# Value rows of an expert layer placed by running sums of work, and a first block that goes ahead to its experts alone

## The chip, the core and the metric

The kernel runs on one core of a Trainium2 chip. The metric is the device time of one execution in microseconds. Five instruction streams run side by side: TensorE (PE in the profile; PEld is its loading of weights), VectorE (DVE), ScalarE (ACT), GpSimd (POOL) and SyncE (SP). Each works through its own instructions in the order in which they stand in the program, and waits for the others by semaphores. Transfers are issued by SP (weights, keys) and by POOL (gathers) and run on 16 DMA engines.

## What is computed

A decoder trunk of two layers over 512 tokens of width 1024. Each layer has a token mixer (differential attention and a recurrent branch, merged and projected), a layer norm, a lookup of experts, and another layer norm:

```python
for l in range(DEPTH):
    mix = token_mixer(x, w_in[l], ..., w_out[l], lam_init)
    x = layer_norm(DEEPNORM_ALPHA * x + mix, ln1_g[l], ln1_b[l])
    ffn = peer(x, peer_wq[l], peer_subkeys[l], peer_u[l], peer_v[l])
    x = layer_norm(DEEPNORM_ALPHA * x + ffn, ln2_g[l], ln2_b[l])

def peer(x, ...):
    q = (xt @ peer_wq).reshape(T, PEER_HEADS, 2, D_KEY_HALF)
    sc = einsum('thcd,hcnd->thcn', q, peer_subkeys)      # 8 heads, two halves of a key
    s1, i1 = top_k(sc[:, :, 0], 16); s2, i2 = top_k(sc[:, :, 1], 16)
    ...                                                  # best 16 of the sums: expert numbers e, weights g
    act = gelu(einsum('cd,ced->ce', xc, take(peer_u, ec)))
    out = einsum('ce,ced->cd', gc * act, take(peer_v, ec))
```

For each token 8 heads choose 16 experts each, so 128 rows of `peer_u` and 128 rows of `peer_v` are read per token and layer.

## The kernel before

**Tiles.** The tokens are four blocks of 128, one token per partition. A dense stage (mixer, then the choice of experts) takes two blocks together: blocks 0 and 1, then 2 and 3, in layer 0 and then in layer 1, so there are four dense stages. The experts run block by block, eight block passes in all, each of 128 gathers. One gather (line 728) brings, for each of the 128 tokens, one row of `peer_u` and the same row of `peer_v`: 1 MB into one of eight buffers `uvt`. The gathers are 1024 in number. They are counted from 0 below, so that gathers 0 to 127 belong to the first block pass, 128 to 255 to the second, and so on.

**One expert row.** VectorE forms the dot product of the token with the u half (line 731), two rows make a pair, ScalarE takes the pair through the gelu (lines 739 and 741), VectorE makes the two weights `w` (lines 743 and 694). Then the v half times its weight is added to the block's result, in one of two ways: VectorE adds it to `acc` (line 701), or ScalarE spreads the weight on a diagonal `dg` (line 705, two buffers) and TensorE multiplies the row with it into `pv` (line 707). Whichever reads the v half last frees the buffer. Which way a row goes is set while the program is written: `used[0]` grows by `self.share` per row, and where it reaches 1 the row goes to VectorE. The share stands in `PLAN` (line 55) for the mixer and for the choice of each dense stage, and is 0.5 where the experts run alone.

**The order.** Three streams are written into one program: `gathers` (experts), `dense` (mixer and choice of a stage) and `late` (the choice for the second block of a stage). `PLAN` gives for each dense stage the gather numbers between which its steps are laid out, so dense work of the next stage stands between the rows of the present block pass. The tile framework then orders the instructions of each engine by that and by the buffers.

**The first dense stage** has no gathers beside it, since the first experts are chosen at its end. Its weights and activations are split into a rounded part and a rest (`hi`, `lo`) and multiplied in three fast passes (`proj_T`, `proj_N`, `split_weight`). Behind the merge of the two branches come, for both blocks together, the output product (`proj_N`, line 550), layer norm (line 559), transposition (line 563) and then `route`: per half key a product with `peer_wq`, also in three passes, a product with the keys (line 587), the best 16 (`top16`) and, after a head, `choose`. `HGS` says how many heads are taken at a time.

## Time and profile before

| what | us |
|---|---|
| median of 3 runs | 3518.49 (3517.03 to 3527.47) |
| the profiled execution | 3519.91 |
| its span | 3518.2 |
| start of the first gather | 317.1 |
| start of the last block pass | 3182.8 |

The page gives busy times of the engines over the whole span. A share of the whole span mixes stages with different limits, so the stretches are what to read: the dense stage without gathers (to 317 us), three mixers beside experts, three ends of a choice beside experts, and the experts alone (from 2843 us). "GB/s" is what all DMA engines moved in a stretch. "PEclk" is the granted TensorE clock of the stretch, as a share of 2.4 GHz.

### The profile page before, as it was taken

To read this page: it belongs to the slowest core of one execution; us is meant where nothing else is said; L and a number is where in the kernel's file an instruction comes from. 1 tells how busy PE (TensorE), PEld (TensorE's weight loads), DVE (VectorE), ACT (ScalarE), POOL (GpSimd) and SP (SyncE) were. 2 spreads that over 40 slices of the span, in tenths; PEclk is the share of its full clock that TensorE was granted. 3 is DMA by queue.
4 is the path that set the end of the run, shared out by engine and by line. 5 is a ranking of instruction groups with operands and counts; after the bars stand their busy time and mean duration, and the time that the engine had idled before them with its cause. 6 is when DMAs were issued, how large, how long until landed. Compare 5 with 4: busy or idle time off the path is not lost.

```text
span 3518.2 us, 38040 instructions
## 1 busy us (share of the span) xinstructions
PE 2743.9 (78%) x11092; PEld 1791.3 (51%) x11092; DVE 2985.2 (85%) x7468; ACT 1267.1 (36%) x3510; POOL 1370.2 (39%) x1033
## 2 busy tenths in 40 slices
PE   8996887799987788896877697798987565556555
PEld 7995555567754365663754264575755221111111
DVE  7765999998799799978799789997789977778777
ACT  7842334443132354423222344443222232223222
POOL 0001234344333443444443434443443445554553
PEclk9997988899998899997989898899989787777776
DMA  5554799999999999999998999999999899999997
GB/s 202 161 168 173 284 379 359 370 415 417 418 402 371 361 405 397 389 418 384 418 395 335 412 399 366 388 402 414 404 410 353 309 374 421 421 421 407 422 421 304
DMA packets 219119, 1290.54 MB, mean 367 GB/s; under 512 B 24592, under 2 KB 37136, under 8 KB 87840
## 3 DMA queue, kind: packets, MB, share of 16 engines
q0 software_dynamic: 147456, 1073.81, 75.8%
q1 hardware_dynamic: 71456, 214.30, 16.2%
q8 instruction: 90, 1.47, 0.2%
q14 instruction: 117, 0.96, 0.1%
HBM read 1285.92 MB, written 2.10 MB: 366 GB/s over the span
## 4 chain that ended last, share of the span: by engine, by line
DVE 37%; PE 25%; DMA 14%; issue 12%; POOL 6%; ACT 6%; POOLq 0%; SPq 0%; DVEq 0%; ACTq 0%
DVE uvt L731 13%; DMA uvt<-uv_dram,e 13%; PE ps_mm L222 12%; DVE acc L701 9%; POOL uvt L728 6%; PE pv L707 6%; PE ps_mm L244 2%; ACT q L741 2%; DVE ef L667 1%; PE ps_ln L299 1%; DVE oh L665 1%; DMA sk<-spk_dram 1%; DVE oh L662 1%; DVE si L627 1%; DVE sc L630 1%
## 5 line engine op out<-in xcount | busy, mean ns | idle before, releaser
L728 POOL DMA_INDIRECT uvt<-uv_dram,e x1024 | 1367.7, 1336 | 2115.7 <-DVE acc L701 985.7
L707 PE MATMUL pv<-uvt,dg 128*128 128x512 f32 x1876 | 1137.7, 746 | 532.7 <-ACT dg L705 531.3
L731 DVE SCALAR_TENSOR_TENSOR uvt<-uvt,xn 128x1024 f32<-128x1024 f32 x1024 | 1243.6, 1219 | 93.7 <-DMA uvt<-uv_dram,e 75.1
L707 PEld LDWEIGHTS pv<-uvt,dg 128*128 128x128 f32 x1876 | 398.4, 229 | 1144.4 <-ACT dg L705 786.0
L222 PE MATMUL ps_mm<-room_xT,w 128*128 128x256 f32 x3072 | 723.1, 385 | 9.7 <-ACT qT L333 4.8
L701 DVE SCALAR_TENSOR_TENSOR acc<-uvt,w,acc 128x1024 f32<-128x1024 f32 x555 | 710.6, 1280 | 9.3
L222 PEld LDWEIGHTS ps_mm<-room_xT,w 128*128 128x128 f32 x3072 | 580.9, 193 | 138.5 <-issue 40.2
L739 ACT ACTIVATE q<-dots 128x2 f32<-128x2 f32 x512 | 103.7, 203 | 1220.5 <-DVE uvt L731 1218.1
L741 ACT ACTIVATE q<-q,dots 128x1 f32<-128x1 f32 x1024 | 341.0, 379 | 14.6
L694 DVE SCALAR_TENSOR_TENSOR w<-q,w 128x2 f32<-128x2 f32 x512 | 80.7, 158 | 233.4 <-ACT q L741 232.0
L705 ACT ACTIVATE dg<-ident,w 128x128 f32<-128x128 f32 x469 | 181.5, 399 | 200.5 <-DVE w L694 180.2
L222 PE MATMUL ps_mm<-room_xT,wsp 128*128 128x256 f32 x768 | 115.2, 293 | 28.7 <-ACT wsp L206 21.8
L207 DVE TENSOR_TENSOR wsp<-raw,wsp 128x1024 fp32r<-128x1024 f32 x96 | 116.2, 1221 | 17.9 <-ACT wsp L206 17.7
L222 PEld LDWEIGHTS ps_mm<-room_xT,wsp 128*128 128x128 f32 x768 | 101.1, 193 | 34.3 <-ACT wsp L206 22.8
L206 ACT CAST wsp<-raw 128x1024 fp32r<-128x1024 f32 x96 | 98.8, 1047 | 26.2 <-issue 7.5
L299 PE MATMUL ps_ln<-lnrows,ident 16*128 16x512 f32 x96 | 65.9, 812 | 39.2 <-DVE w L743 22.8
L244 PEld LDWEIGHTS ps_mm<-w,room_xT 128*128 128x128 f32 x768 | 90.6, 192 | 7.5 <-issue 4.8
L244 PE MATMUL ps_mm<-w,room_xT 128*128 128x128 f32 x768 | 92.7, 276 | 0.4 <-ACT tha L454 0.3
L244 PEld LDWEIGHTS ps_mm<-w,room_m 128*128 128x128 f32 x768 | 88.0, 192 | 7.3 <-issue 4.8
L222 PE MATMUL ps_mm<-room_ya,w 128*128 128x256 f32 x384 | 90.0, 382 | 1.5 <-DVE mth L506 1.2
L350 PE MATMUL s<-kT,qT 64*128 64x256 f32 (+1 forms) x384 | 71.1, 407 | 24.8 <-DVE pr L354 21.1
L244 PE MATMUL ps_mm<-w,room_m 128*128 128x128 f32 x768 | 88.6, 275 | 1.8 <-DVE room_m L510 1.1
(193 smaller groups left out, 2967.5 us busy)
## 6 DMA issues: line engine op xcount, KB each, us to landing
w<-wpk_dram SPq DMA_DIRECT2D x288, 512.0 KB, 8.3
raw<-wpk_dram SPq DMA_DIRECT2D x96, 512.0 KB, 4.4
uvt<-uv_dram,e POOLq DMA_INDIRECT x1024, 11.4
gw<-gpk_dram SPq DMA_DIRECT2D x32, 128.0 KB, 6.8
sk<-spk_dram SPq DMA_DIRECT2D x64, 64.0 KB, 7.1
xn<-x_dram SPq DMA_DIRECT2D x4, 512.0 KB, 4.0
out_dram<-xn SPq DMA_DIRECT2D x8, 256.0 KB, 6.1
lq<-lqk_dram SPq DMA_DIRECT2D x2, 128.0 KB, 6.7
```

The costliest lines, as they stand in the source:

```text
L206: self.nc.scalar.copy(hi, raw)
L207: self.nc.vector.tensor_tensor(lo, raw, hi.bitcast(F32), ALU.subtract)
L222: self.nc.tensor.matmul(ps[:, :n], w, x, start=i == 0, stop=i == len(steps) - 1)
L244: self.nc.tensor.matmul(out[:, i], x(slice(i * P, (i + 1) * P)), w, start=j == 0, stop=j == len(steps) - 1)
L299: nc.tensor.matmul(ps[:, half], self.ident[:16, r : r + 1].to_broadcast([16, P]), self.lnrows, start=True, stop=True)
L701: nc.vector.scalar_tensor_tensor(out=acc, in0=t[:, D:], scalar=w[:, i : i + 1], in1=acc, op0=ALU.mult, op1=ALU.add)
L705: nc.scalar.activation(dg, self.ident, AF.Copy, scale=w[:, i : i + 1])
L707: nc.tensor.matmul(pv[:, half], dg, t[:, D + half * 512 : D + (half + 1) * 512], start=not used[1], stop=j == P - 2)
L728: nc.gpsimd.indirect_dma_start(out=t, out_offset=None, in_=self.uv, in_offset=bass.IndirectOffsetOnAxis(ap=e[:, j : j + 1], axis=0))
L731: nc.vector.scalar_tensor_tensor(out=t[:, :D], in0=t[:, :D], scalar=C_GELU, in1=x, op0=ALU.mult, op1=ALU.mult, accum_out=dots[:, i : i + 1])
L739: nc.scalar.activation(q, dots, AF.Square, scale=A_GELU / C_GELU)
L741: nc.scalar.activation(q[:, k : k + 1], q[:, k : k + 1], AF.Tanh, scale=dots[:, k : k + 1], bias=dots[:, k : k + 1])
```

## The change

**Placement of value rows.** The shares in `PLAN` and the counter `used[0]` are gone. A class `Load` walks over the instructions written so far and keeps running sums for TensorE, VectorE and DMA, each instruction with a price by its size. DMA sets a floor: neither engine's sum may fall more than 8 us behind the sum of DMA, and the sum of DMA not more than 12 us behind the larger of the two. A row goes to VectorE where VectorE's sum plus 1.22 us is not above TensorE's sum plus 1.72 us. In the built order 699 of the 1024 rows go to TensorE in place of 469. VectorE keeps 325 in place of 555.

**First block alone.** In the first dense stage `first_experts` takes the place of the shared tail. The output weights are split for all eight chunks ahead, into all eight buffers of the gathers. The norm's scale and shift rows are brought by TensorE ahead of the product, into two PSUM tiles. Then block 0 goes alone through product, norm, transposition, the scores of head 0 and its choice. Block 1 follows with the same weights.

**Keys in float32.** The activations for the scores of that stage are kept in one float32 copy, and `peer_wq` is read as it is: 8 passes of float32 in place of 24 of the split form per half key, and no splitting of these 16 weight chunks.

```diff
-    (0, [2, 3], 30, 222, 270, 370, (0.7, 0.25)),
+    (0, [2, 3], 30, 222, 270, 370),
...
-V_ALONE = 0.5
...
-HGS = {True: (1, 1, 2, 2, 2), False: (2, 2, 2, 2)}
+HGS = {True: (1, 2, 2, 2), False: (2, 2, 2, 2)}
...
+class Load:
+    SLACK, AHEAD = 8.0, 12.0
...
+            if inst.engine == mybir.EngineType.PE:
+                self.pe += 0.013 + n / 2400 if inst.ins[0].dtype == F32R else 0.009 + n / 596
+            elif inst.engine == mybir.EngineType.DVE:
+                n = max([n] + [size(o) for o in inst.ins if hasattr(o, "ap")])
+                self.dve += 0.15 + n / 960 + 0.08 * (len(inst.outs) > 1 or "Match" in name)
+            elif name == "InstDMACopy":
+                self.dma += n * min(P, list(inst.outs[0].ap)[0][1]) * 4 / 420e3
+                self.dma = max(self.dma, max(self.pe, self.dve) - self.AHEAD)
+                self.pe = max(self.pe, self.dma - self.SLACK)
+                self.dve = max(self.dve, self.dma - self.SLACK)
...
+    def first_experts(self, l, blocks, m, sums):
+        nc = self.nc
+        affine = [self.norm_rows(l, 0, 0, self.ps_s, "s2"), self.norm_rows(l, 0, 1, self.ps_v, "pv")]
+        junk = self.ap.tile([P, D], F32, name="junk", tag="ya")
+        wts = []
+        for c in range(0, KC, 2):
+            t = [self.gp.tile([P, 2, D], F32R, name="wsp", tag="uv") for _ in range(2)]
+            for a in range(2):
+                self.split_weight(t[0][:, a], t[1][:, a], l, CH_OUT + c + a)
+            wts.append([v.rearrange("p a (k c) -> p a k c", k=KC) for v in t])
+        self.acts_x = Acts(self.room("xT"))
+        w = sk = None
+        for i, b in enumerate(blocks):
...
+            self.layer_norm(l, 0, [(b, sums[:, i, :2])], 4.0 * LN_EPS, junk, affine)
+            self.transpose_x(self.acts_x, i, b)
...
+            for c in range(2):
+                yield from self.score(l, c, w[c], sk[c], [i], sc)
+                o = [sv, si] if i == 0 else self.top
+                self.top16([(sc[i][:, c], o[0][:, c], o[1][:, c])])
+            if i == 0:
+                yield from self.choose(l, 0, 1, sv, si, b)
...
-                used[0] += self.share
-                if j == P - 1 or (used[0] >= 1.0 and j < P - 2):
-                    used[0] -= 1.0
+                self.load.update()
+                vector = self.load.dve + 1.22 <= self.load.pe + 1.72
+                if j == P - 1 or (vector and j < P - 2):
```

TensorE at the end of the first dense stage, before. The names: `wsp` are split weights, `room_uv` the merged activations, `ps_ln` the norm's rows, `ps_xt` the transposition (`xn_103` blocks 0 and 1, `xn_4775` blocks 2 and 3 of the next stage), `ps_sc` the scores.

```order
L244 MATMUL ps_mm<-wsp,room_uv 128x256 x192
L299 MATMUL ps_ln<-lnrows,ident 128x512 x2
L272 MATMUL ps_xt<-ident,xn_103 128x128 x16
L222 MATMUL ps_mm<-room_xT,wsp 128x256 x8
L222 MATMUL ps_mm<-room_kT_117,wsp 128x256 x8
L222 MATMUL ps_mm<-room_xT,wsp 128x256 x8
L272 MATMUL ps_xt<-ident,xn_4775 128x128 x4
L587 MATMUL ps_sc<-sk,pqT 128x128 x2
L222 MATMUL ps_mm<-room_xT,wsp 128x256 x8
```

The same place after; the merged activations are now in `room_yr` and `room_xn`, and `ps_mm<-room_xT,w` is the float32 product for a half key.

```order
L628 MATMUL ps_mm<-wsp,room_yr 128x256 x16
L628 MATMUL ps_mm<-wsp,room_xn_2612 128x256 x8
L628 MATMUL ps_mm<-wsp,room_yr 128x256 x8
L305 MATMUL ps_xt<-ident,xn_103 128x128 x8
L665 MATMUL ps_mm<-room_xT,w 128x128 x8
L672 MATMUL ps_sc<-sk,pqT 128x128
L665 MATMUL ps_mm<-room_xT,w 128x128 x8
L672 MATMUL ps_sc<-sk,pqT 128x128
L628 MATMUL ps_mm<-wsp,room_yr 128x256 x8
L628 MATMUL ps_mm<-wsp,room_xn_2612 128x256 x8
```

The 192 products of both blocks were one row; now block 0's 96 end in the first three rows, its transposition and both scores follow, and block 1's product comes behind them.

TensorE in the first mixer of layer 1 (beside block pass 2, gathers from 256), before. `pv` are value rows (two products a row), `s`, `pt` and `po` attention, the other rows dense products.

```order
L707 MATMUL pv<-uvt,dg 128x512 x2
L222 MATMUL ps_mm<-room_xT,w 128x256 x4
L244 MATMUL ps_mm<-w,room_xT 128x128 x16
L350 MATMUL s_10149<-kT_104,qT 128x128
L222 MATMUL ps_mm<-room_xT,w 128x256 x16
L707 MATMUL pv<-uvt,dg 128x512 x2
L222 MATMUL ps_mm<-room_xT,w 128x256 x8
L350 MATMUL s_10366<-kT_104,qT 128x256 x2
L376 MATMUL pt<-ident,pr 128x128
L381 MATMUL po<-vn_105,pr 128x128
L707 MATMUL pv<-uvt,dg 128x512 x2
```

The same place after.

```order
L807 MATMUL pv<-uvt,dg 128x512 x4
L277 MATMUL ps_mm<-w,room_xT 128x128 x3
L807 MATMUL pv<-uvt,dg 128x512 x4
L277 MATMUL ps_mm<-w,room_xT 128x128 x6
L388 MATMUL s_10054<-kT_104,qT 128x128 x2
L255 MATMUL ps_mm<-room_xT,w 128x256 x3
L807 MATMUL pv<-uvt,dg 128x512 x4
L255 MATMUL ps_mm<-room_xT,w 128x256 x7
L807 MATMUL pv<-uvt,dg 128x512 x4
L255 MATMUL ps_mm<-room_xT,w 128x256 x5
L807 MATMUL pv<-uvt,dg 128x512 x4
```

Where one row of the experts stood between some 24 dense products, two now stand between three to eleven.

VectorE at the same place, before. `dots` is line 731, `acc` a value row, `pr` and `at_st` the softmax.

```order
L354 SCALAR_TENSOR_TENSOR pr<-base,s_10366 128x2x256
L694 SCALAR_TENSOR_TENSOR w<-q,w 128x2
L625 MAX tv<-ca 128x8
L701 SCALAR_TENSOR_TENSOR acc<-uvt,w,acc 128x1024
L731 SCALAR_TENSOR_TENSOR uvt,dots<-uvt,xn_4775 128x1024
L359 TENSOR_REDUCE at_st<-pr 128x2
L465 SCALAR_TENSOR_TENSOR mu<-mu,tl 128x256
L360 TENSOR_SCALAR at_st<-at_st 128x2
L625 MAX tv<-ca 128x8
L627 MAX_INDEX pi<-tv,ca 128x8
L731 SCALAR_TENSOR_TENSOR uvt,dots<-uvt,xn_4775 128x1024
```

The same place after.

```order
L834 SCALAR_TENSOR_TENSOR uvt,dots<-uvt,xn_4441 128x1024 x2
L846 TENSOR_TENSOR w<-dots,g_114 128x2
L794 SCALAR_TENSOR_TENSOR w<-q,w 128x2
L392 SCALAR_TENSOR_TENSOR pr<-base,s_10289 128x2x256
L834 SCALAR_TENSOR_TENSOR uvt,dots<-uvt,xn_4441 128x1024
L397 TENSOR_REDUCE at_st<-pr 128x2
L503 SCALAR_TENSOR_TENSOR mu<-mu,tl 128x256
L398 TENSOR_SCALAR at_st<-at_st 128x2
L509 SCALAR_TENSOR_TENSOR thx<-thx,xc 128x256
L762 TENSOR_TENSOR oh<-iota,pf 128x864
```

The value row is gone from between the dot products.

## Rows read from the trace of the kernel before

**Rows 1.** Page: span; busy us, share of the span, instructions of an engine
```profile
span 3518.2 us, 38040 instructions
...
PE 2743.9 (78%) x11092; PEld 1791.3 (51%) x11092; DVE 2985.2 (85%) x7468; ACT 1267.1 (36%) x3510; POOL 1370.2 (39%) x1033
```

**Rows 2.** Busy time by stretch of gathers: engines, TensorE clock, DMA share, GB/s
```profile
317.00:445.00 128.00, 99.33 (x490) 69.94 (x491) 105.41 (x419) 45.20 (x127) 37.67 (x32) 0.88 0.83 308
445.00:766.00 321.00, 260.18 (x1127) 186.52 (x1126) 309.96 (x767) 144.09 (x390) 126.41 (x96) 0.89 0.96 378
766.00:979.00 213.00, 200.00 (x984) 154.90 (x983) 170.75 (x352) 62.94 (x180) 89.32 (x65) 0.99 1.02 418
979.00:1188.00 209.00, 165.62 (x512) 94.13 (x511) 197.80 (x691) 62.12 (x203) 88.54 (x64) 0.88 0.94 373
1188.00:1445.00 257.00, 209.36 (x818) 140.99 (x819) 233.95 (x585) 119.70 (x330) 101.23 (x80) 0.89 0.99 397
1445.00:1756.00 311.00, 267.26 (x1176) 194.14 (x1174) 247.49 (x510) 95.71 (x282) 134.93 (x96) 0.90 1.00 404
1756.00:2002.00 246.00, 181.22 (x540) 101.81 (x540) 223.57 (x729) 68.67 (x227) 104.67 (x80) 0.89 0.96 378
2002.00:2312.00 310.00, 244.76 (x1001) 167.10 (x1000) 283.92 (x647) 138.24 (x371) 131.24 (x96) 0.89 0.98 387
2312.00:2573.00 261.00, 241.20 (x1148) 184.61 (x1148) 213.75 (x430) 80.85 (x235) 108.53 (x81) 0.96 1.01 410
2573.00:2843.00 270.00, 190.69 (x536) 102.26 (x534) 259.16 (x881) 73.36 (x239) 106.99 (x81) 0.83 0.90 346
2843.00:3486.00 643.00, 386.27 (x546) 122.98 (x544) 506.22 (x901) 172.39 (x525) 337.68 (x256) 0.76 1.01 418
```

**Rows 3.** Busy time of three shorter stretches, the same columns
```profile
88.00:176.00 88.00, 86.97 (x692) 81.89 (x691) 66.97 (x148) 71.57 (x156) 0.00 (x0) 1.00 0.50 161
792.00:880.00 88.00, 87.54 (x404) 66.75 (x403) 76.28 (x154) 32.99 (x94) 40.45 (x28) 1.00 1.02 418
1936.00:2024.00 88.00, 58.28 (x104) 22.30 (x105) 67.65 (x151) 28.65 (x85) 42.92 (x36) 0.88 1.01 413
```

**Rows 4.** Groups by line: busy us, mean ns, idle before and its releasers
```profile
L701 DVE SCALAR_TENSOR_TENSOR acc<-uvt,w,acc 128x1024 f32<-128x1024 f32 x555 | 710.6, 1280 | 9.3
...
L705 ACT ACTIVATE dg<-ident,w 128x128 f32<-128x128 f32 x469 | 181.5, 399 | 200.5 <-DVE w L694 180.2 <-PE pv L707 11.7 <-DVE e L670 5.5
```

**Rows 5.** Timeline, TensorE around 760 us: start, duration, count
```profile
755.23 1.88 PE L707 MATMUL pv<-uvt,dg 128*128 128x512 f32 x4
...
756.95 1.50 PE L244 MATMUL ps_mm<-w,room_xT 128*128 128x128 f32 x12
...
768.13 7.17 PE L222 MATMUL ps_mm<-room_xT,w 128*128 128x256 f32 x32
```

**Rows 6.** Timeline, from the first output product past the first gather
```profile
262.02 21.62 PE L244 MATMUL ps_mm<-wsp,room_uv 128*128 128x256 f32 x178 [0.82 <-ACT room_uv L258]
...
288.68 3.78 PE L299 MATMUL ps_ln<-lnrows,ident 16*128 16x512 f32 x4 [5.05 <-DVE xn L306]
...
292.50 2.47 DVE L306 SCALAR_TENSOR_TENSOR xn<-xn,ln_st,ps_ln 128x1024 f32<-128x1024 f32 x2 [3.44 <-PE ps_ln L299]
...
298.14 2.08 PE L222 MATMUL ps_mm<-room_xT,wsp 128*128 128x256 f32 x8
...
307.68 0.29 DVE L625 MAX8 sv<-sc 128x8 f32<-128x128 f32 x1 [1.58 <-ACT sc L594]
...
317.11 1.09 POOL L728 DMA_INDIRECT uvt<-uv_dram,e  x1 [313.96 <-DVE sm_st L675]
...
342.44 1.11 PE L222 MATMUL ps_mm<-room_kT,wsp 128*128 128x256 f32 x8
```

**Rows 7.** Waits from 440 to 704 us: total us, times, longest
```profile
POOL uvt L728 <- DVE acc L701: 63.1, 23, 5.1
...
PE pv L707 <- ACT dg L705: 24.9, 9, 6.3
```

More of the change, by code (lines that the diff above doesn't have):

```diff
@@ L77, in weave, with __init__, begin, update @@
             yield c
+class Load:
+    SLACK, AHEAD = 8.0, 12.0
+    def __init__(self, nc):
+        self.nc = nc
+        self.seen = 0
+        self.begin()
+    def begin(self):
+        self.pe = self.dve = self.dma = 0.0
+    def update(self):
+        todo = self.nc.cur_bb.bb.instructions
+        for inst in todo[self.seen :]:
+            name = type(inst).__name__
+            if not inst.outs or not hasattr(inst.outs[0], "ap"):
+                continue
+            size = lambda o: math.prod(n for _, n in list(o.ap)[1:])
+            n = size(inst.outs[0])
+            if inst.engine == mybir.EngineType.PE:
[8 more added lines that the diff above has]
+                self.dve = max(self.dve, self.dma - self.SLACK)
+        self.seen = len(todo)
 class Acts:
@@ L275, in transpose_x, with norm_rows, layer_norm @@
                       ps.rearrange("p (k t) -> p k t", k=4))
-    def layer_norm(self, l, which, rows, eps, junk):
+    def norm_rows(self, l, which, v, pool, tag):
+        ps = pool.tile([P, 2, 512], F32, name="ps_ln", tag=tag)
+        for half in range(2):
+            r = l * 8 + which * 4 + v * 2 + half
+            self.nc.tensor.matmul(ps[:, half], self.ident[:16, r : r + 1].to_broadcast([16, P]),
+                                  self.lnrows, start=True, stop=True)
+        return ps
+    def layer_norm(self, l, which, rows, eps, junk, affine=None):
         nc, t2 = self.nc, self.t2
@@ L295, in layer_norm @@
         for v, (col, op0, op1) in enumerate(((1, ALU.add, ALU.mult), (3, ALU.mult, ALU.add))):
-            ps = self.ps_s.tile([P, 2, 512], F32, name="ps_ln", tag="s2")
-            for half in range(2):
-                r = l * 8 + which * 4 + v * 2 + half
-                nc.tensor.matmul(ps[:, half], self.ident[:16, r : r + 1].to_broadcast([16, P]),
-                                 self.lnrows, start=True, stop=True)
+            ps = affine[v] if affine else self.norm_rows(l, which, v, self.ps_s, "s2")
             for (b, _), st in zip(rows, sts):
@@ L577, in route @@
+    def route(self, l, blocks, h0):
+        if h0 == 0:
+            self.begin_top()
+        for HG in HGS[h0 > 0]:
             sv, si = self.top_tiles(HG)
             for hc in range(2 * h0, 2 * (h0 + HG)):
-                sk = t2.tile([P, 2, P], F32, name="sk", tag="gs")[:, 0]
-                nc.sync.dma_start(sk, self.spk[l, hc])
-                pq = self.proj_T(l, CH_WQ + hc, self.acts_x, n)
-                qT = t2.tile([P, MAXN], F32, name="pqT", tag="row", bufs=5)
-                nc.scalar.copy(qT[:, :n], pq[:, :n])
@@ L584, in route @@
-                yield nb * C_CHUNK
-                ps = self.ps_mm.tile([P, 512], F32, name="ps_sc", tag="mm")
-                for i in range(nb):
-                    nc.tensor.matmul(ps[:, i * P : (i + 1) * P], qT[:, i * P : (i + 1) * P], sk,
-                                     start=True, stop=True)
                 c = hc % 2
                 if c == 0:
-                    sc = [t2.tile([P, MAXN], F32, name="sc", tag="row", bufs=5)
-                          .rearrange("p (c k) -> p c k", c=2) for i in range(nb)]
@@ L593, in route @@
-                for i in range(nb):
-                    nc.scalar.copy(sc[i][:, c], ps[:, i * P : (i + 1) * P])
-                yield 0.5
+                    sc = {}
+                sk = self.subkeys(l, hc)
+                yield from self.score(l, hc, self.weight(l, CH_WQ + hc), sk,
+                                      list(range(len(blocks))), sc)
                 if c:
@@ L689, in experts @@
         e, g = self.e[b], self.g[b]
-        used = [0.0, False]
+        began = [False]
         def finish(j0, q, w, uvs):
@@ L708, in finish @@
                                          t[:, D + half * 512 : D + (half + 1) * 512],
-                                         start=not used[1], stop=j == P - 2)
-                    used[1] = True
+                                         start=not began[0], stop=j == P - 2)
+                    began[0] = True
             yield
@@ L759, in run @@
         self.done = set()
-        self.share = 0.5
+        self.load = Load(nc)
         def gathers():
@@ L776, in dense @@
         def dense():
-            for k, (l, blocks, j0, j1, j2, _, shares) in enumerate(PLAN):
+            for k, (l, blocks, j0, j1, j2, _) in enumerate(PLAN):
                 if l:
@@ L785, in dense @@
                     yield ("chosen", k - 1)
-                self.share = shares[1]
-                yield from paced(self.route(l, blocks), 16 * nb * C_CHUNK + 24 + choice, j1, j2)
+                yield from paced(self.route(l, blocks, int(k == 0)), 16 * nb * C_CHUNK + 24 + choice, j1, j2)
                 self.done.add(("scored", k))
-            self.share = V_ALONE
         def late():
-            for k, (l, blocks, _, _, j2, j3, _) in enumerate(PLAN):
+            for k, (l, blocks, _, _, j2, j3) in enumerate(PLAN):
                 yield ("scored", k)
```

77 lines of the change are left out of this document (61 added, 16 removed), and 3 rows, old and new, of the table PLAN.

## Prediction

> **What bounds the kernel now.** I read the busy times by stretch first, then the price of single rows, then the chain at the start, then the waits. The page gives VectorE 85% and TensorE 78% of the span [rows 1], which names no bound, since the stretches differ [rows 2]. From 2843 us the experts run alone at 418 GB/s: there the gathers themselves are the limit, and 418 is my figure for what the DMA engines can do. The three mixers beside experts (445 to 979, 1188 to 1756, 2002 to 2573 us; gathers 32 to 191, 256 to 431, 512 to 687) take 534, 568 and 571 us. Their first parts are below that limit: 378, 397 and 387 GB/s, with VectorE busy 97%, 91% and 92% of the time. Their second parts run at 404 to 418 GB/s with VectorE at 80%. The three ends of a choice (979 to 1188, 1756 to 2002, 2573 to 2843) run at 346 to 378 GB/s with VectorE at 95%, 91% and 96%. So VectorE is what holds the gathers back, by some tens of us in each stage. The waits agree: POOL waited 63.1 us in 440 to 704 us for a buffer that VectorE's value row had yet to release [rows 7]. Ahead of all that stand 317 us without a gather [rows 6].
>
> TensorE has room in the mixers, but how much? Its busy time times its granted clock is about its work at full clock: 260.2 x 0.89 + 200.0 x 0.99 = 430 us of 534; 427 of 568; 449 of 571 [rows 2].
>
> **Moving rows, prices.** A row on VectorE is 1.28 us [rows 4]. On TensorE it is 1.72 us at full clock, from the start of one row to the next instruction (755.23 to 756.95 us) [rows 5], and twice that at the lower of its two clock levels. On ScalarE it adds a `dg` of 0.40 us [rows 4]; 230 of them are 92 us on an engine that is busy 36% [rows 1], hidden beside the dot products. By stretch I counted the value rows of the built order: in the three mixers VectorE loses 46, 66 and 59 rows, in the three choice ends 7, 10 and 10, in the experts alone 31, before 445 us one: 230.
>
> **Mixers.** VectorE falls by 46, 66 and 59 times 1.28, that is 59, 84 and 76 us, from 481, 481 and 498 to about 422, 397 and 422: it is no longer the limit. The DMA needs 210.4, 227.7 and 227.0 MB at 418 GB/s: 503, 545 and 543, together 1591. TensorE gets 79, 114 and 101 us more: 509, 540 and 551, together 1600, and 4 for the keys (below): 1604. So what is late next is TensorE, nearly level with the DMA. What share of the time can it work? In the first dense stage, without gathers, 86.97 of 88 us at full clock, 98.8%; beside gathers at 418 GB/s 87.54 of 88 in 792 to 880 us [rows 3], and 94% in 766 to 979 us [rows 2], where it was not the limit. But there five value rows of sixteen were its own, now up to fifteen, and each waits for a chain over three engines. I take 97%, nearer to the stretches in which it was full: 1604 / 0.97 = 1654 against 1673, a gain of 19. At 99% it is 53, at 92% a loss of 70. The mixer's size is therefore one number, TensorE's fill, and it decides the sign.
>
> **Choice ends.** 27 rows are 35 us less on VectorE. The built order also lets some dense work of the mixers slide later, so that by its count VectorE's work there falls by 20 us only, and part of that is where the DMA is the limit. I take 14; the bounds are 5 and 37 (35 / 0.94).
>
> **Experts alone.** 31 rows go to TensorE, most at the start of block pass 6. Nothing is won, since the DMA is the limit. The cover is that TensorE is idle there 40% of the time at clock 0.76 [rows 2]; a stretch with most rows on TensorE (1936 to 2024) moved 413 GB/s [rows 3]. If the cover fails, for some 60 gathers a row at the lower clock (3.44 us) is longer than a gather (1.05 MB at 418 GB/s, 2.5 us): some 55 us at most, unlikely since the stretches with a full TensorE were granted 1.00 [rows 3].
>
> **First block alone.** From the start of the output product (262.02) to the first gather (317.11) are 55.1 us [rows 6]. The product of both blocks is 21.6; block 1's half, 11, goes behind. The norm's second rows were made by TensorE behind the first step, 288.68 to 292.50; that 3.8 is gone, but the rows now stand ahead of the product and cost about 1 more than the wait that covers them. The second block's square and row steps leave about 1.2. The scores, from 298.14 to 307.68 (9.5), are two products of 16 passes of 128 columns, each 1.8 at full clock (half of 0.224 a pass [rows 5]), twice at the lower level, and the copies between: 7 to 9, so 2 less. The choice (9.4) stays. Sum: 17 earlier, first gather near 300 us. Behind the first gather now stand block 1's norm, transposition and scores, and VectorE is the limit from there to 445 us (105.4 of 128 busy). I give back 3 and take 14. Bounds: 5 and 20. The covers: the eight gather buffers hold the split weights until block 1's product has read them; it starts near 290 and gives up the first two buffers 3 us later at full clock, well before the choice ends (if it runs at the lower level throughout, up to 10 us of the gain are gone). VectorE's step on block 1's product stands ahead of the cast of the expert numbers `e`: 0.7 us if the product is ready. SP's load of the next blocks' `xn` now waits for block 1's product, because the merged rest lies there, and holds back weights and keys queued behind it; by the built order they are first used behind block 1's scores, which are later still. ScalarE's and VectorE's splitting of eight weight chunks moves ahead, beside a stage in which TensorE is full and VectorE busy 76% [rows 3]; without that cover it would be 10 us.
>
> **Keys in float32.** Per half key 24 fast passes at 1.11 for 8 (2.9 us net of overlap) [rows 6] become 16 of 0.224 (3.6): 14 x 0.6 = 8 us more on TensorE up to about 500 us, half of it counted above, half before 445 us beside VectorE. VectorE and ScalarE lose 16 splits of about 1.2 and 1.0 us; VectorE's 19 us pay for block 1's steps.
>
> Sum: 14 + 19 + 14 = 47 from the profiled execution's 3519.9 (its span 3518.2; the median of the runs is 3518.5): 3473.
>
> **Rivals.** (1) *The mixers give nothing.* TensorE reaches 95%: 1688, a loss of 15; with 28 from the other two terms 3507. For it: the counter prices TensorE at full clock, while the mixers were granted 0.89 to 0.99, and VectorE by a formula that over the built order of before gives 3343 us where the page shows 2985. Both errors send too many rows to TensorE. (2) *TensorE becomes a bound that is worse than VectorE was.* Place: the mixers, where a pair of value rows now stands between few dense products. In 440 to 704 us TensorE waited 24.9 us for `dg` [rows 7], in which it had some 30 rows: 0.8 us a row. If each of the 171 rows moved in the mixers brings that wait, 137 us are added to TensorE's 1604, a fill of 92%: a loss of 70, less 17 of the other two terms at their poorer ends: 3573. It decides below 94%. Against it: the waits were seen where TensorE had work left over; an engine that is behind finds its inputs ready. The clock falls with idling: in experts alone, with TensorE busy 60%, 0.76 was granted [rows 2]. The Trainium skill, "TensorE: Matmul & The Clock Gate", section "HAM oscillation", says the same, that repeated gaps let the clock drop to half; by that rule such waits cost more than their length and the time would lie above 3573, and the trace agrees as far as the clock goes. (3) *TensorE isn't near its limit.* Its weight loads were busy 154.9 of 213 us, 73%, in 766 to 979 us [rows 2]. If that is its fill, the mixers go to the DMA's 1591 / 0.99 = 1607, a gain of 66, VectorE's relief in the choice ends counts in full (37) and the start gives 20: 3397. The Trainium skill, "Perfetto Trace Analysis", section "Identifying the Most-Contended Engine", wants TensorE judged so, not by matmul busy time. Against it: 32 passes of 256 columns took 7.17 us, back to back [rows 5], and a value row's passes are 512 columns for the same load of weights, so loads may be idle where products aren't. (4) *The change doesn't do what it says* is the counter's error in (1); it has no chance of its own.
>
> **How the numbers follow.** Forecast 3473, for 3440 to 3500: 0.52. Rival 1, 3500 to 3530: 0.20. Rival 2, above 3530: 0.14. Rival 3, below 3440: 0.14. 0.3% (10.6 us) is about what a measurement of this kernel can tell from no change. Faster (below 3508): 0.52 + 0.14 + 0.09 = 0.75; same: 0.11; slower: 0.14. The range leaves out rival 2 and the far part of rival 3: 3415 to 3530.
>
> **What would show it.** First gather near 300 us; VectorE below 85% in the mixers and TensorE above 95% at a clock near 1.0, with 395 to 410 GB/s; POOL's waits for buffers now ended by TensorE's value rows instead of VectorE's. Wrong would be: TensorE waiting for `dg` as long as before per row, a clock below 0.9 in the mixers, VectorE still at 95%, or a first gather later than 312.

## The result

| | us |
|---|---|
| before, median of 4 runs | 3520.97 (3517.03 to 3527.47) |
| after, median of 4 runs | 3466.73 (3463.7 to 3472.31) |
| ratio | 0.9846, 95% interval 0.9825 to 0.9867 |
| profiled execution after | 3468.77, span 3466.6 |

The change takes 54 us off, 47 to 62 by the interval. The forecast was 3473, 47 below the profiled execution of the kernel before.

The page of the kernel after, the rows that answer to [rows 1] and [rows 4]: span, busy time of an engine, then groups by line (busy us, mean ns | idle before).

```profile
span 3466.6 us, 39937 instructions
...
PE 2996.7 (86%) x11916; PEld 1916.2 (55%) x11916; DVE 2717.2 (78%) x7210; ACT 1329.1 (38%) x3730; POOL 1303.2 (38%) x1033
...
L807 PE MATMUL pv<-uvt,dg 128*128 128x512 f32 x2796 | 1448.5, 657 | 355.2 <-ACT dg L805 352.6
...
L801 DVE SCALAR_TENSOR_TENSOR acc<-uvt,w,acc 128x1024 f32<-128x1024 f32 x325 | 416.6, 1282 | 7.8
L805 ACT ACTIVATE dg<-ident,w 128x128 f32<-128x128 f32 x699 | 263.0, 397 | 261.8 <-DVE w L794 154.5
```

VectorE lost 230 value rows and TensorE got them; the two have changed places in busy time. How the stretches of [rows 2] look now, between the same gathers (0, 32, 128, 192, 256, 336, 432, 512, 608, 688, 768, 1023):

```profile
299.00:427.00 128.00, 109.30 (x444) 77.67 (x444) 104.22 (x476) 38.87 (x126) 35.09 (x32) 0.93 0.87 329
427.00:730.00 303.00, 292.97 (x1252) 198.67 (x1251) 264.98 (x682) 154.79 (x426) 121.04 (x97) 1.00 0.99 398
730.00:936.00 206.00, 200.87 (x922) 151.47 (x921) 159.68 (x323) 63.62 (x187) 84.08 (x64) 0.99 1.02 418
936.00:1153.50 217.50, 184.35 (x659) 110.90 (x658) 192.87 (x705) 68.53 (x215) 81.11 (x65) 0.93 0.96 377
1153.50:1412.00 258.50, 247.22 (x886) 152.32 (x885) 183.78 (x515) 121.09 (x342) 91.18 (x81) 0.96 0.97 384
1412.00:1715.00 303.00, 301.83 (x1335) 217.87 (x1334) 219.60 (x495) 107.99 (x328) 120.79 (x96) 1.00 1.01 411
1715.00:1965.00 250.00, 201.28 (x618) 109.17 (x617) 217.05 (x740) 76.37 (x244) 103.97 (x80) 0.91 0.97 383
1965.00:2269.00 304.00, 290.79 (x1113) 182.86 (x1111) 234.35 (x591) 146.64 (x403) 115.25 (x96) 0.98 0.99 390
2269.00:2524.00 255.00, 253.19 (x1157) 187.17 (x1154) 199.47 (x413) 90.83 (x262) 105.34 (x80) 1.00 1.01 416
2524.00:2792.00 268.00, 213.12 (x693) 120.06 (x692) 249.35 (x881) 79.20 (x250) 104.23 (x80) 0.89 0.92 354
2792.00:3435.00 643.00, 409.90 (x675) 140.48 (x673) 468.38 (x868) 181.46 (x554) 337.48 (x256) 0.82 1.01 418
```

In the six rows of the mixers TensorE is now busy 95.6% to 99.6% of the time at a clock of 0.96 to 1.00, and VectorE 71% to 87%. Set against [rows 2]:

| | before | after | change | forecast |
|---|---|---|---|---|
| to the first gather | 317.1 | 298.7 | -18.4 | -17 |
| first gather to gather 32 | 128.0 | 128.3 | 0 | +3 |
| three mixers | 1673 | 1629.5 | -43 | -19 |
| three choice ends | 725 | 735.5 | +10 | -14 |
| experts alone | 643 | 643 | 0 | 0 |

The sum is close to the forecast, and two terms of it are off by 24 us each, in opposite directions. The start of the kernel after (start, duration, engine, line):

```profile
261.11 2.07 PE L628 MATMUL ps_mm<-wsp,room_yr 128*128 128x256 f32 x8
...
274.82 0.69 DVE L631 SCALAR_TENSOR_TENSOR xn<-xn,ps_mm 128x512 f32<-128x512 f32 x1 [4.96 <-PE ps_mm L628]
...
277.34 1.27 DVE L344 SCALAR_TENSOR_TENSOR xn<-xn,ln_st,ps_ln 128x1024 f32<-128x1024 f32 x1
...
278.98 1.28 DVE L344 SCALAR_TENSOR_TENSOR xn<-xn,ln_st,ps_ln 128x1024 f32<-128x1024 f32 x1
...
282.17 3.78 PE L665 MATMUL ps_mm<-room_xT,w 128*128 128x128 f32 x16
...
286.69 1.95 PE L665 MATMUL ps_mm<-room_xT,w 128*128 128x128 f32 x16
...
298.74 1.09 POOL L831 DMA_INDIRECT uvt<-uv_dram,e  x1 [295.60 <-DVE sm_st L775]
```

Block 0's product ends near 274.8, the norm's second row step (278.98) comes without a wait for `ps_ln`, and the two score products cost 3.78 us at a granted clock of 0.50 and 1.95 us at 1.00, as taken in the prediction. Two steps have other sizes than its working gives. Block 0's product took 13.7 us (261.11 to 274.82), where half of 21.6 was taken; its first products ran at a granted clock of 0.50 (261 to 263 us). Norm and transposition, from the end of the product to the scores, took 7.4 us where [rows 6] has 14.5, so 7 us went and not 4. The two errors nearly cancel: 18 us against the 17 of the working.

The waits turned as well. POOL's waits for a buffer in the first part of the first mixer, 427 to 730 us (total us, times, longest), and TensorE's there:

```profile
POOL uvt L831 <- PE pv L807: 100.7, 42, 6.5
POOL uvt L831 <- DVE acc L801: 17.1, 8, 4.7
...
PE pv L807 <- ACT dg L805: 4.5, 4, 1.7
```

In [rows 7] VectorE's rows ended most of these waits. That they are TensorE's now, as the prediction said, holds for the first part of each mixer only. In the second parts VectorE's rows still end more (98.4 us against 60.6 from 1412 to 1715 us). Over the six stretches of the mixers TensorE's rows ended 439 us of waits and VectorE's 326, where before it was 144 and 617. TensorE waited 4.5 us for `dg`, where [rows 7] has 24.9 in a shorter stretch with far fewer rows on TensorE.

### The profile page after: what moved, and what is told of

It is laid out like the page before. It is cut to its first block, busy times and chain, and to the rows that moved or that the text cites. A ratio compares the mean times of both kernels' runs of the same rounds, so it can differ in the third digit from the quotient of the medians.

```text
span 3466.6 us, 39937 instructions
## 1 busy us (share of the span) xinstructions
PE 2996.7 (86%) x11916; PEld 1916.2 (55%) x11916; DVE 2717.2 (78%) x7210; ACT 1329.1 (38%) x3730; POOL 1303.2 (38%) x1033
## 4 chain that ended last, share of the span: by engine, by line
PE 36%; DVE 25%; DMA 19%; issue 9%; ACT 5%; POOL 5%; POOLq 0%; SPq 0%; DVEq 0%; ACTq 0%
DMA uvt<-uv_dram,e 19%; PE ps_mm L255 14%; PE pv L807 13%; DVE uvt L834 9%; POOL uvt L831 5%; DVE acc L801 4%; PE ps_mm L277 2%; ACT q L844 1%; PE ps_mm L665 1%; DVE oh L765 1%; PE ps_ln L315 1%; DVE ef L767 1%; DVE oh L762 1%; PE s L388 1%; PE po L419 1%
## 5 line engine op out<-in xcount | busy, mean ns | idle before, releaser
L831 POOL DMA_INDIRECT uvt<-uv_dram,e x1024 | 1300.6, 1270 | 2132.0 <-PE pv L807 721.5
L807 PE MATMUL pv<-uvt,dg 128*128 128x512 f32 x2796 | 1448.5, 657 | 355.2 <-ACT dg L805 352.6
L807 PEld LDWEIGHTS pv<-uvt,dg 128*128 128x128 f32 x2796 | 541.2, 205 | 1081.3 <-ACT dg L805 576.9
L255 PE MATMUL ps_mm<-room_xT,w 128*128 128x256 f32 x2304 | 538.4, 381 | 0.7 <-ACT room_xT L287 0.7
L255 PEld LDWEIGHTS ps_mm<-room_xT,w 128*128 128x128 f32 x2304 | 431.4, 190 | 107.1 <-issue 50.3
L801 DVE SCALAR_TENSOR_TENSOR acc<-uvt,w,acc 128x1024 f32<-128x1024 f32 x325 | 416.6, 1282 | 7.8
L805 ACT ACTIVATE dg<-ident,w 128x128 f32<-128x128 f32 x699 | 263.0, 397 | 261.8 <-DVE w L794 154.5
L665 PE MATMUL ps_mm<-room_xT,w 128*128 128x256 f32 (+1 forms) x1056 | 243.5, 379 | 0.0
L665 PEld LDWEIGHTS ps_mm<-room_xT,w 128*128 128x128 f32 x1056 | 196.5, 196 | 46.2 <-issue 23.8
L846 DVE TENSOR_TENSOR w<-dots,g 128x2 f32<-128x2 f32 x512 | 80.1, 157 | 17.3 <-ACT dg L805 4.3
L255 PE MATMUL ps_mm<-room_yr,w 128*128 128x256 f32 x384 | 90.6, 380 | 0.0
## 6 DMA issues: line engine op xcount, KB each, us to landing
gw<-gpk_dram SPq DMA_DIRECT2D x32, 128.0 KB
lq<-lqk_dram SPq DMA_DIRECT2D x2, 128.0 KB
```

The source lines that it names most:

```text
L255: self.nc.tensor.matmul(ps[:, :n], w, x, start=i == 0, stop=i == len(steps) - 1)
L665: nc.tensor.matmul(pq[:, :n], w[:, kc, :], self.acts_x.plain[:, kc, t0 : t0 + n], start=kc == 0, stop=kc == KC - 1)
L801: nc.vector.scalar_tensor_tensor(out=acc, in0=t[:, D:], scalar=w[:, i : i + 1], in1=acc, op0=ALU.mult, op1=ALU.add)
L805: nc.scalar.activation(dg, self.ident, AF.Copy, scale=w[:, i : i + 1])
L807: nc.tensor.matmul(pv[:, half], dg, t[:, D + half * 512 : D + (half + 1) * 512], start=not began[0], stop=j == P - 2)
L831: nc.gpsimd.indirect_dma_start(out=t, out_offset=None, in_=self.uv, in_offset=bass.IndirectOffsetOnAxis(ap=e[:, j : j + 1], axis=0))
```

## The experiments

All times are medians beside runs of the kernel before on the same chip, whose medians were 3522.4, 3522.9, 3517.5 and 3521.8 in the four groups. A gain is 1 less the ratio, times that median, with its 95% interval.

### The two halves of the change apart

The start alone (the kernel after, rows placed by the old counter):

```diff
-                self.load.update()
-                vector = self.load.dve + 1.22 <= self.load.pe + 1.72
+                used[0] += self.share
+                vector = used[0] >= 1.0
...
```

> The kernel after with the placement of value rows undone: shares in PLAN and the counter as before (555 rows on VectorE). First block alone and float32 keys stay. Theory (start and placement are separate terms, and the start is kept): first gather at 299 us, 18 earlier than before; the lead at gather 32 still 14 to 18; no further change behind it; 3500 to 3506, a gain of 14 to 19. Rival (VectorE, the limit up to gather 32, takes the start back, and what the kernel after keeps of it is owed to the placement): lead below 8 at gather 32 and 3512 to 3520.

3496.84 us, ratio 0.9925: a gain of 26 us (22 to 31), more than either theory. First gather at 298.0, lead at gather 32 (how much earlier it starts than in the kernel before, at 445.1) 15.4.

The placement alone (the kernel before, with `Load`):

> The kernel before with the placement alone: class Load decides each value row; start, split keys and HGS as before. Theory (additive): first gather at 317 us; the three mixers gain 42 together, the three choice ends lose 10; 3485 to 3490, a gain of 30 to 35, which with e_start sums to the whole change's 52. Rival (the placement's gain needs VectorE's relief by the float32 keys or the earlier start): a gain below 22, above 3498.

3491.32 us, ratio 0.9905: a gain of 33 us (28 to 39). In its trace the first gather is at 319.3, the mixers take 1637 and the choice ends 734.5. The two gains sum to 60, the whole change gave 54: within the intervals they add up. The placement is worth what the prediction gave it, 19 + 14 = 33. The start is worth about 26 where it gave 14.

### What in the start gains

The start has two parts, keys in float32 and block 0 alone. The keys alone, in the kernel before:

```diff
+        if split:
+            x = self.acts_x = Acts(self.room("xT"))
         for i, b in enumerate(blocks):
             self.transpose_x(x, i, b)
```

> The kernel before with float32 keys alone: the activations for the scores of the first dense stage in one float32 copy, peer_wq unsplit; both blocks together and the shares as before. Theory (the prediction's): the scores before the first gather take as long as before within 2 us, first gather at 315 to 319; TensorE 8 us more and VectorE 19 less up to about 500 us; 3513 to 3522, no measurable change. Rival (splitting the keys is what held the gathers up to 445 us): lead of 8 or more at gather 32 and 3505 to 3512.

3495.92 us, ratio 0.9921: a gain of 28 us (23 to 32), where the prediction had the keys down as a cost. The first gather came 3 us later than before (320.2) and gather 32 came 20.4 us earlier. So the part that was to gain, block 0 alone, is not needed for it. What the keys do shows in POOL's waits of the kernel before, 317 to 445 us:

```profile
POOL uvt L728 <- DVE sm_st L675: 314.0, 1, 314.0
POOL uvt L728 <- PE pv L707: 28.7, 10, 10.3
POOL uvt L728 <- PE ps_mm L222: 15.3, 4, 5.9
```

The third row is a gather that waits for a dense product. The split weights of a half key lie in a buffer of the pool from which the gathers take theirs (`wsp`, tag "uv"), and it comes free when the product has read it. To tell the buffers from the splitting work on VectorE, the splits were kept and put elsewhere, in the kernel before:

```diff
-            t = self.gp.tile([P, 2, D], F32R, name="wsp", tag="uv")
+            if ch >= CH_WQ:
+                t = self.ap.tile([P, 2, D], F32R, name="wsp", tag=("ya", "m")[ch % 2])
+            else:
+                t = self.gp.tile([P, 2, D], F32R, name="wsp", tag="uv")
```

> The kernel before, where the split weights of the 16 half keys lie in two rooms of the mixer that are free by then, and no longer in the gather buffers. Everything else, the 16 splits on VectorE and ScalarE too, as before. The float32 keys alone moved gather 32 from 445 to 424 us; this run asks by what. Theory (the buffers: a gather had to wait until the products of a half key had released its buffer): lead of 12 to 20 at gather 32 and 3498 to 3508. Rival (VectorE's 14 splits of 1.22 us behind the first gather, 17 us, were the delay): lead below 5 and 3517 to 3525.

3500.15 us, ratio 0.9942: a gain of 20 us (15 to 26), from moving tiles to free memory, with all the work kept; gather 32 came 15.9 us earlier. POOL's wait for `ps_mm` between gathers 0 and 32 (320 to 429 us) fell to this row:

```profile
POOL uvt L731 <- PE ps_mm L225: 0.8, 1, 0.8
```

The buffers are most of what the keys gained. The 7 us between the two runs may be VectorE's splits, but their intervals overlap. Then block 0 alone, with split keys in free rooms (the kernel after, old placement):

> The kernel after with the old shares and with split keys (24 fast passes, hi and lo of the weights in two free rooms): the first block alone is then the only change. Theory (VectorE's splits are the delay, and the block alone only moves the first gather): first gather at 299 to 303 us, but the lead at gather 32 below 5, 3515 to 3523. Rival (the buffers are the delay, and are out of the way here too): lead of 15 to 20 at gather 32, 3496 to 3506, like the start with float32 keys.

3507.11 us, ratio 0.9959: a gain of 14 us (9 to 20), first gather at 303.1, lead at gather 32 11.1: between the two theories, nearer to the rival. Since the buffers are out of the way here too, it is to be held against the run before it, which gained 20 with its first gather at 322.8. Block 0 alone added nothing to that. The same with everything else as in the kernel after, that is the kernel before with the keys and the placement (its text takes gains as differences of medians, 26 and 25 us, where the ratios gave 28 and 26):

> The kernel before with float32 keys and the placement by Load, without the first block alone: the kernel after less that one part. Theory (the freed gather buffers, not the earlier first gather, are what the start is worth: the keys alone gave 26 us, block alone with the keys 25): first gather at 319 to 321 us, lead at gather 32 as in the kernel after, 18 to 21; 3463 to 3470, the same as after. Rival (the earlier first gather is worth its 18 us once VectorE is relieved): 3478 to 3488.

3460.77 us, ratio 0.9833 (0.982 to 0.9847): a gain of 59 us (54 to 63), not told apart from the kernel after (54). It is the shortest of the versions that compute everything. From the first gather to gather 32, the kernel after and this one:

```profile
298.50:427.00 128.50, 109.80 (x449) 78.17 (x448) 104.65 (x478) 38.87 (x126) 35.35 (x32) 0.93 0.87 328
...
319.50:420.00 100.50, 90.38 (x327) 57.30 (x327) 91.02 (x399) 28.65 (x106) 36.43 (x33) 1.00 1.00 400
```

The kernel after leads by 21 us at the first gather and still at gather 8, by 2 us at gather 16, and is 7 us behind at gather 32. Block 1's product, norm and scores, which stood ahead of the first gather, now stand in this stretch, and it is 28 us longer. TensorE's busy time up to gather 32 is the same in both, 386 us. I then tried to use the early gathers by choosing two heads for block 0 first:

```diff
-            for c in range(2):
-                yield from self.score(l, c, w[c], sk[c], [i], sc)
...
+            for h in range(2):
...
+                for c in range(2):
+                    hc = 2 * h + c
...
+                    yield from self.score(l, hc, self.weight(l, CH_WQ + hc), sk, [i], sc)
```

> The kernel after, with heads 0 and 1 scored and chosen for block 0 ahead of block 1's product and norm (the four weight chunks are read a second time for block 1). Theory (the lead of 25 us at gather 8 falls to 13 at gather 16 because gathers 16 to 31 wait for head 1's choice, which stands behind block 1's norm and scores): first gather 298 to 300 us, gather 16 up to 15 us earlier than in the kernel after (345 to 355 us), but gather 32 waits for heads 2 and 3 behind the same work: lead there 15 to 25, 3460 to 3470. Rival (the DMA engines, idle 10 to 20% until gather 32, keep what gather 16 gains): lead of 30 or more at gather 32, 3450 to 3458.

3468.51 us, ratio 0.9863 (0.9845 to 0.9881), no gain. Gather 16 came at 374.4, not at 345 to 355 and 13 us later than in the kernel after, and gather 32 at 435.2. Both theories missed gather 16. Its wait isn't for the choice of head 1, whose expert numbers were written at 306.73 us. It is for buffers:

```profile
306.73 0.17 DVE L769 CAST e<-ef 128x16 int32<-128x16 f32 x1
...
342.03 1.02 PE L806 MATMUL pv<-uvt,dg 128*128 128x512 f32 x2
342.89 0.61 PE L671 MATMUL ps_sc<-sk,pqT 128*128 128x128 f32 x4
343.33 3.62 PE L664 MATMUL ps_mm<-room_xT,w 128*128 128x256 f32 x16
346.79 1.02 PE L806 MATMUL pv<-uvt,dg 128*128 128x512 f32 x2
...
348.08 1.27 POOL L830 DMA_INDIRECT uvt<-uv_dram,e  x1 [8.36 <-PE pv L806]
```

A whole value row is four records on TensorE ([rows 5]); here only two stand together, half a row, and the other half comes behind the next half key's product and scores. Gathers 11, 12 and 13 (338.8, 348.1, 357.6 us) each start 0.3 us after a second half, so TensorE frees a buffer only every 9 us or so. The kernel after has the same order: up to gather 32, 16 of its 22 groups of value products are not whole rows, against 2 of 13 in the version without the first block alone. That this order costs the whole lead is not shown, since no run kept the halves together.

### What bounds the kernel now

First VectorE's side. 39 value rows of the choice ends go to TensorE:

```diff
+                n = (4 * l + b) * P + j
+                vector &= not any(a <= n < a + 64 for a in (192, 448, 704))
```

> The kernel after, with no value row on VectorE in the gathers 192 to 255, 448 to 511 and 704 to 767 (39 rows more on TensorE, the last row of a block stays). Theory (VectorE sets the pace in the choice ends, since it was busy 30.0 of 30 us in four slices from 1010 to 1130 us, and TensorE had some 30 us at full clock left in each): 39 x 1.28 = 50 us less on VectorE, of which up to 15 per end come back; 3425 to 3450. Rival (the choice ends are longer because dense work that TensorE didn't do in the mixer slid into them, and TensorE is the limit there as well): 39 x 1.72 = 67 us more on TensorE, no gain or a loss; 3465 to 3490.

3467.75 us, the kernel after to within 1 us. Its three choice ends:

```profile
931.50:1143.00 211.50, 198.76 (x719) 119.31 (x718) 160.47 (x608) 70.87 (x224) 71.20 (x64) 0.98 0.98 386
...
1711.00:1959.50 248.50, 210.97 (x657) 115.88 (x656) 202.82 (x722) 79.22 (x256) 98.63 (x80) 0.97 0.97 384
...
2521.00:2790.00 269.00, 231.51 (x740) 129.90 (x740) 235.67 (x868) 81.78 (x262) 102.39 (x81) 0.91 0.92 354
```

VectorE fell from 659 to 599 us over the three, the time from 735.5 to 729, and the mixers took 7 more. My theory, that VectorE alone sets the pace there, fell. Then rows the other way, back to VectorE, by a dearer TensorE in `Load`:

```diff
-                self.pe += 0.013 + n / 2400 if inst.ins[0].dtype == F32R else 0.009 + n / 596
+                self.pe += 0.013 + n / 2400 if inst.ins[0].dtype == F32R else 0.018 + n / 550
```

> The kernel after with TensorE's float32 price in Load raised from 0.009 + n/596 to 0.018 + n/550 us: 414 value rows go to VectorE in place of 325, half of the 89 in the mixers. Theory (TensorE is late last in the mixers and its work sets the end): 89 x 1.72 = 153 us less on TensorE, 114 more on VectorE, which has room in the mixers (70 to 88%): a gain of 5 to 20, 3447 to 3462. Rival (the limit is shared, rows moved back to VectorE cost as much there as TensorE gains): 3462 to 3480.

3469.05 us, ratio 0.9846: no change again. The trace counts 394 value rows on VectorE, 69 more than in the kernel after and not 89, and 52 of these are in the mixers. With 286, 325 or 394 rows on VectorE the time is the same within the intervals; with the old shares (the start alone, 558 in its trace) it is 28 us longer by the ratios. It is a plateau, and the counter's errors in price, which the first rival of the prediction rested on, cost nothing on it. No run gave the old counter a lower share, so it is not shown that the running sums do better than a lower fixed share would.

From gather 32 to gather 768 all three take 2365 us. What changes is how it divides: 1629.5, 1636.5 and 1641.5 us in the mixers, 735.5, 729 and 723.5 in the choice ends. The stretches are cut at gather numbers, and dense work slides across the cuts: with 394 rows on VectorE the mixers moved 664 MB and the choice ends 263, in the kernel after 655 and 272.

Next TensorE's work by itself: the second half of the product of nearly every TensorE value row is left out, the placement stays.

```diff
                     for half in range(2):
+                        if half and began[0] and j < P - 2:
+                            self.load.pe += 0.009 + 512 / 596
+                            continue
```

> The kernel after with the second half of each TensorE value row's product left out (but for the first and the last row of a block); the sums of Load count it as if it were there, so that the rows stay where they are. TensorE loses some 680 x 0.86 = 585 us at full clock. Theory (TensorE is late last in the mixers, at 96% fill): the mixers fall from 1629 to the DMA's 1591 or VectorE's needs, 1595 to 1605, and the choice ends by up to 30; 3405 to 3440. Rival (TensorE is not the limit; VectorE, the buffers or the DMA are): 3455 to 3470.

3461.02 us, 6 us below the kernel after (7 by the ratios, and the intervals overlap). Four of its stretches, mixers and the last choice end:

```profile
426.00:727.00 301.00, 285.53 (x1314) 210.23 (x1313) 259.48 (x669) 156.20 (x437) 117.84 (x96) 0.98 1.00 409
727.00:950.50 223.50, 185.58 (x835) 136.09 (x834) 168.76 (x384) 68.20 (x190) 87.59 (x64) 0.86 0.96 388
...
1408.00:1712.00 304.00, 247.78 (x999) 167.38 (x998) 211.80 (x453) 95.03 (x275) 123.19 (x97) 0.83 0.99 403
...
2518.50:2780.50 262.00, 159.80 (x458) 88.61 (x456) 241.31 (x850) 71.99 (x239) 99.92 (x81) 0.75 0.90 345
```

TensorE's busy time multiplied by its granted clock, summed over mixers and choice ends, fell from 2113 to 1653 us, and the time of these nine stretches from 2365 to 2354.5. Again the parts moved against each other: the choice ends fell to 702.5 us, and the mixers, which were to gain, grew to 1652 and moved 667 MB. So TensorE's fill, on which the prediction built the mixers, is not by itself what holds them. The clock went down with the work: 1.00 to 0.83 in the stretch from gather 336, which is still 304 us long. With both engines relieved (the same cut, and every value row but a block's last on TensorE):

> The kernel with half of each TensorE value row's product left out (as in the run before this with that cut, but for the first and last row of a block), and with all value rows but the last of a block on TensorE, so both engines are relieved at once: VectorE by 317 x 1.28 = 406 us. Cutting TensorE's work by 460 us at full clock moved the stretch from gather 32 to 767 by 10 of 2365 us only. Theory (in the mixers the gathers are at what the DMA engines do beside weights, 402 to 405 GB/s, DMA share 0.99 to 1.01; in the choice ends VectorE, 88 to 93% busy, sets the pace): mixers 1615 to 1640, the three choice ends 735 shrink by 30 to 60; 3400 to 3435. Rival (VectorE holds the mixers too, through the order of its work): mixers 1590 to 1605; 3370 to 3400. Second rival (eight buffers and the length of the chain from landing to release): no change beyond 10, 3450 to 3465.

3410.43 us, ratio 0.9695, 51 us below the run before it (46 by the ratios): relief of VectorE gives some 50 us once TensorE has room, and gave none above, where its rows went to a TensorE without room. Its three choice ends:

```profile
931.50:1124.00 192.50, 140.66 (x441) 80.03 (x440) 163.15 (x653) 61.70 (x214) 73.24 (x64) 0.88 0.97 386
...
1677.00:1919.00 242.00, 178.95 (x563) 99.16 (x562) 191.90 (x717) 81.41 (x266) 88.45 (x80) 0.87 0.98 397
...
2474.00:2729.50 255.50, 178.88 (x595) 102.30 (x594) 220.27 (x848) 81.36 (x268) 94.65 (x80) 0.88 0.92 363
```

They take 690 in place of 735.5 in the kernel after, the mixers 1614.5 in place of 1629.5. Against the run before it, 37.5 of the 50 us come from the mixers and 12.5 from the choice ends, where the theory had VectorE set the pace. The mixers of the kernel after are thus within 15 us of what both engines' relief gives. No run relieved VectorE alone, with TensorE's rows left as they are. That the rest is the DMA, as their share near 1.0 suggests, was tested by leaving out every second load of a weight chunk as well:

```diff
+        if ("scored", 0) in self.done and self.calls % 2:
...
+            return self.last_w
         w = self.last_w = self.wp.tile([P, KC, P], F32, name="w", tag="w")
```

> The run before this with both engines relieved (half of the product of the TensorE value rows left out, no value row on VectorE but a block's last), and here every second load of a weight chunk left out as well, from the second dense stage on: two chunks' products use the same weights. Some 120 of 240 chunks of 0.52 MB, 63 MB, 150 us at 418 GB/s. Theory (with the engines relieved, the mixers' 1614 us at 405 to 413 GB/s are what the DMA engines need): the mixers fall by 60 to 120, until TensorE's 1450 at full clock stand in the way; the choice ends, with VectorE 79 to 86% busy, by 0 to 30; 3270 to 3345. Rival (the DMA share near 1.0 only shows queued gathers, and the chain over three engines with eight buffers sets the pace): within 20 of 3410.

3397.26 us, 13 us below the run before it (18 by the ratios): my theory fell. The mixers moved 605 MB in place of 660, 130 us less at 418 GB/s, and took 1603. Three of their rows:

```profile
424.50:722.50 298.00, 290.17 (x1303) 207.08 (x1303) 231.96 (x645) 162.32 (x459) 111.40 (x96) 1.00 0.97 376
722.50:929.00 206.50, 199.15 (x898) 142.35 (x897) 117.58 (x306) 77.73 (x220) 69.22 (x64) 0.98 0.93 367
...
1379.50:1666.50 287.00, 259.39 (x1055) 176.30 (x1054) 153.92 (x390) 97.81 (x304) 101.96 (x96) 0.93 0.98 390
```

In the first of them TensorE is again busy 97% at full clock: dense work has moved into the place of the missing products, 1303 records of matmuls where the kernel after has 1252. In the third no engine is full. What keeps the mixers at 1600 us here is open. The order of TensorE's queue, in which a value row that frees a buffer stands behind dense products, and the eight buffers are candidates; neither was tried.

## Why the prediction was right, and where not

**The total** was right (3473 against 3467), the sign and the likeliest case too. Its steps did less well than the sum, and that the sum came out so close is partly luck: mixers and choice ends were off by 24 us each and cancelled, and the start got its gain from another part than the one it was put down to.

**First block alone, 14.** The first gather came at 298.7 as worked out, with two steps of other sizes that nearly cancel. The claim that 14 of 17 us stay did not hold: the keys alone gained as much as the whole start, and the kernel after gained no more than its like without this part. The failing sentence is "I give back 3". Held against that version, all 21 us were given back before gather 32, and 7 more: what stood ahead of the first gather now stands behind it, and TensorE's value rows stand in halves between its products.

**Keys in float32, a small cost set against VectorE's relief.** This was the step that failed most. The keys alone gained 28 us. I priced instructions (TensorE 8 us more, VectorE 19 less) and not the memory they use: fourteen split chunks took turns with the gathers in eight buffers. The row that tells it (POOL waiting for `ps_mm`, 15.3 us) is in the trace of before, in a stretch whose waits the prediction does not use. So the start was put at 14 for one part and nothing for the other. It is worth 26, and the other part alone gives 28.

**Mixers, 19, and choice ends, 14.** Together 33 were forecast, and the placement alone measured 33. Apart they were wrong: 43 and -10. The term that was mis-sized is TensorE's work in the mixers. 1604 us were summed and 1569 are there (busy time multiplied by granted clock, the six rows of the mixers). The choice ends have 544 where [rows 2] gives 465 and the 27 moved rows add 46: 33 us of dense work slid into them from the mixers. The weights show the same: the mixers moved 655 MB against 665 before, the choice ends 272 against 265. The prediction saw the sliding for VectorE in the built order and did not carry it to TensorE. The fill came out at 1569 / 1629.5 = 96.3% against the 97% taken; but this number isn't the cause of the time by itself, since 460 us less of TensorE's work left the stretches about as long. What the runs show is weaker: after the change, moving rows between TensorE and VectorE does nothing, relieving TensorE alone gave 6 us, within the intervals, and both 56. That the two hold mixers and choice ends together is argued from this, since VectorE alone was not relieved. The step "it is no longer the limit" was too strong for VectorE: in the second part of each mixer POOL still waits more for its rows than for TensorE's.

**Experts alone, 0.** 642.8 and 642.7 us from gather 768 to 1023: the cover held, at a clock of 0.82.

**Rivals.** Rival 2, TensorE waiting 0.8 us a row for `dg`, fell: the waits for `dg` come to 17.5 us in the six stretches of the mixers together; of the 352.6 us over the span (the page's group L807) 222.8 lie in the experts alone, where TensorE is idle 36% of the time. The clock in the mixers rose to 0.96 to 1.00. By the rule on oscillation that the prediction weighed (the Trainium skill, "TensorE: Matmul & The Clock Gate", section "HAM oscillation") such waits would have cost the clock too; the waits did not come, and where the halved products left gaps the trace agrees with the rule (0.83 in the stretch from 1408 us, with TensorE busy 82% of the time). Rival 3, TensorE far from its limit, gave 3397; the run with both engines relieved, 3410, shows what such a time needs. Rival 1, the counter's errors in price, met a plateau. As for DMA, the Trainium skill, "Perfetto Trace Analysis", section "Identifying the Most-Contended Engine", says that DMA is to be judged by the bandwidth reached and not by occupancy. The trace agrees: with half of the weights' transfers gone the mixers had shares of 0.93 to 0.98 at 367 to 390 GB/s, against 0.99 to 1.01 at 405 to 413.

## What to carry to other kernels

Price the memory of a step as well as its instructions: tiles that take turns with a prefetch in one pool hold the prefetch back, and the row to look for is the issuing engine waiting for an instruction of another job. A first item that comes earlier is worth only what the items behind it keep, so follow the lead past the second and third item before counting it, and see whether the instructions that free a buffer stay together in their engine's order. Stretches that are cut at gather numbers trade work with each other, so judge a change by their sum before reading one of them. Where two engines can do the same work, balance them until moving a share either way changes nothing; from there relieving one gained 6 us here and relieving both 56.

## What was not expected of the hardware

The granted TensorE clock fell when TensorE's work was made lighter. Leaving out 460 us of TensorE's work (at full clock) between gathers 32 and 768 lowered its busy time there by 308 us only, 2186 to 1877, and the clock of the whole span fell from 0.94 to 0.82. Whether the lower clock cost time is not shown.

A DMA share near 1.0 does not say that the DMA engines limit a stretch: with 8% fewer bytes in the mixers (605 MB for 660) the share fell by 0.01 to 0.08 and the time by 0.7%.
